# S5's matrices B turned by eight transposes of 128 rows, turned feed-forward rows copied out of PSUM first, and the last product in banks of its own

## The chip, the core and the metric

The kernel runs on one core of a Trainium2 chip. The core has five engines that run side by side and wait for each other through semaphores: TensorE (PE in the profile; its weight loads are listed apart as PEld) multiplies and transposes and writes to PSUM, ScalarE (ACT) and VectorE (DVE) work elementwise on PSUM and on the on-chip memory SBUF, GpSimd (POOL) works elementwise on SBUF and issues transfers, and SyncE (SP) issues transfers. PSUM has eight banks; a bank holds 512 float32 values in each of 128 partitions. The metric is the time of one execution on the device, in microseconds (us); lower is better.

## What is computed

One encoder layer in float32: 512 tokens of 1024 channels, 256 memory tokens, a feed-forward width of 2816. Cut to what matters here:

```python
def s5_scan(u, lam_re, lam_im, log_step, b_re, b_im, c_re, c_im, reverse):
    ...
    b = lax.complex(b_re.astype(f32), b_im.astype(f32))
    b_bar = ((lam_bar - 1.0) / lam)[..., None] * b
    bu = jnp.einsum('gpc,lbgc->lbgp', b_bar, u.astype(jnp.complex64))
    ...

def reference(...):
    ...
        n = rms_norm(h, mix_norm_g[i])
        proj = n @ w_in[i]
        ya = s5_branch(...)          # S5, two directions, 32 groups, 64 states, 16 channels
        yb = sgu_branch(...)
        merged = gate_a * (ya @ w_proj_a[i]) + gate_b * (yb @ w_proj_b[i])
        h = h + merged @ w_out[i]
        h = h + memory_cross_attention(rms_norm(h, xattn_norm_g[i]), memn, ...)
        h = h + swiglu(rms_norm(h, ffn_norm_g[i]), w_gate[i], w_up[i], w_down[i])
    return rms_norm(h, final_norm_g)
```

S5's matrices B come as `b_re` and `b_im` of shape (2 directions, 32 groups, 64 states, 16 channels); `swiglu` is `(silu(hn @ w_gate) * (hn @ w_up)) @ w_down`.

## The kernel before

Everything is float32 but runs through TensorE in a faster format in two parts: `split` (line 83) makes of a matrix a high part `hi` (a cast by ScalarE, line 85) and a low part `lo` (source minus `hi`, VectorE, line 86), and each product is three matmuls: hi*hi, hi*lo, lo*hi (`mm3`, line 371). Weights come in blocks of 512 KB from a list, `plan`: loaded by SyncE three and more blocks ahead into three buffers `raw` (line 145 and others), split two blocks ahead into three buffers each of `whi` and `wlo`. A large part of the big products is done by a scheme with seven half-size products (numbered `q` = 1 to 7, weights and activations added up beforehand).

Order. The program is written as one stream. When it is built, a planner that simulates a timeline of the engines (`schedule_with_timeline_sim=True`) puts the instructions of each engine into an order; each engine and each transfer queue then works in that fixed order. Where the code says `in_order` (or sets `pinned`), the order written stands. Small jobs are put between the products by `later` and by a generator `s5_program`, which `tick` moves on.

PSUM is two pools: five banks `mm` for products (`bank`), three banks `aux` for small results and transposes (`aux`), each handed out in turn.

Three places matter here.

**S5's setup** (`s5_setup`, from line 688), early in the kernel while the first product (`pt`, token rows times `w_in`) runs. `brow` holds B with 64 rows (real and imaginary part, 32 groups) of direction, state and channel; for each of the 16 channels one transpose (line 726) turns 64 rows by 128 columns (a step of 16 elements between the columns) into 128 by 64, eight to a bank `pbc`, and ScalarE copies each bank to `raw_b` (line 727). The loads of `brow` (line 716) stand in SyncE's queue ahead of those of `crow` (C's matrices, line 720) and of the next blocks of `w_in` (line 145).

**The turning of rows for the feed-forward part.** After the attention's output product (`pt`, lines 1664 to 1688), each of the four row blocks of 128 tokens is normalised (`scale_row`, giving `xs`; the factor `r` is a power taken on GpSimd, line 511) and turned by `turn_row`, which calls `to_feat` (line 528): per half (`q` = 0, 1) four transposes into one `aux` bank `ptr` (line 534), then `split` from that bank into `fn_hi` and `fn_lo`, then ScalarE copies the bank to `full` (line 540). `full` is later used to add up activations for the products 5, 6 and 3. For rows 0 and 1 the transposes are `turned`: they stand in the written order between the products of rows 2 and 3, in the loop of lines 1684 to 1686. There are four half rows for three banks, so the second half of row 1 uses the bank of the first half of row 0.

**The last product and the output.** The down product (`w_down`) runs in the order q = 1, 5, 2, 6, 3, 7, 4 (`DOWN`, line 260), each in six chunks of weights, in two banks `dx`, `dq` or `dv` for the two row blocks of a half of the tokens. `onto_h` (line 1931) adds a finished pair of banks onto the residual `h`. Products 1, 6, 7 and 4 pile up in `dx`: after product 7, `onto_h(dx, 2, 0, SUBTRACT)` (line 1953) takes `dx` off the first column half of rows 2 and 3, and product 4 goes on adding into the same banks, which later go onto their second half (line 1971 for row 2; `seed_last`, line 1900, for row 3). The first three chunks of product 4 do both rows; the last three (`held`) do row 2, then row 3 in two parts of 256 columns. Finished halves are multiplied by the gain ahead of time into `hg` (four rows of 512, in `rest`; `first_half`, line 1874), so that at the end only one factor per token is left: for the last row `write` (line 1915) scales 512 columns on ScalarE and stores them from SyncE's queue (line 1924), and scales the other 512, which lie in `h`, on VectorE and stores them from ScalarE's queue (lines 1926 and 1929).

Of the kernel before, what the change touches and what calls it, by code (L numbers as in the profile page):

```python
# [9 lines left out]
F32 = mybir.dt.float32  # L10
F32R = mybir.dt.float32r
AF = mybir.ActivationFunctionType
ALU = mybir.AluOpType
# [4 lines left out]
P = 128  # L18
D = 1024
T = 512  # L20
NT = T // P
# [5 lines left out]
G = 32  # L27
C = 16
# [24 lines left out]
def hybrid_layer_kernel(  # L53
# [8 lines left out]
    nc = tc.nc  # L62
# [17 lines left out]
    def aux(name, shape=(P, 512)):  # L80
        return pa.tile(list(shape), F32, tag="aux", name=name)

    def split(dst_hi, dst_lo, src):

        hi = nc.scalar.copy(dst_hi, src)  # L85
        lo = nc.vector.tensor_tensor(dst_lo, src, dst_hi.bitcast(F32), ALU.subtract)  # L86
        if pinned[0]:
            in_order(hi)
            in_order(lo)
        return hi  # L90
# [434 lines left out]
        for i in range(2):  # L525
            nc.vector.scalar_tensor_tensor(dst[:, HALF[i]], src[:, HALF[i]], r, g[:, HALF[i]], ALU.mult, ALU.mult)

    def to_feat(src, hi, lo, tsl, full=None, skip=None, part=(0, 1), turned=False):

        for q in part:  # L530
            ps = aux("ptr", (P, 4, P))
            for j in range(4):
                k = 4 * q + j
                m = nc.tensor.transpose(ps[:, j, :], src[:, k * P:(k + 1) * P], ident)
                if turned:
                    in_order(m)
            if q != skip:
                split(hi[:, 4 * q:4 * q + 4, tsl], lo[:, 4 * q:4 * q + 4, tsl], ps)
            if full is not None:
                nc.scalar.copy(full[:, 4 * q:4 * q + 4, tsl], ps)  # L540

    xsp = [None]
# [145 lines left out]
    def s5_setup():  # L688
# [22 lines left out]
        yield 0.3  # L711


        brow = s5p.tile([2 * G, 2, 64, C], F32, tag="u", name="brow")
        for i, src in enumerate((s5_b_re, s5_b_im)):
            nc.sync.dma_start(brow[G * i:G * i + G], src[0].rearrange("d g p c -> g d p c"))
        crow = s5p.tile([P, 2, C // 4, 2, 64], F32, tag="tt", name="crow")
        for i, src in enumerate((s5_c_re, s5_c_im)):
            for d in range(2):
                nc.sync.dma_start(crow[:, i, :, d, :], src[0, d].rearrange("g (a b) p -> (g a) b p", a=4))  # L720
        bb = s5p.tile([P, 2, G, C], F32, tag="raw_b", name="raw_b")
        rows = brow.rearrange("g d p c -> g (d p) c")
        for n in range(2):
            ps = aux("pbc", (P, C // 2, 2 * G))
            for k in range(C // 2):
                nc.tensor.transpose(ps[:, k, :], rows[:, :, 8 * n + k], ident[:2 * G, :2 * G])
            A_.copy(bb.rearrange("p i g c -> p c (i g)")[:, 8 * n:8 * n + 8, :], ps)
            yield None
        cc = s5p.tile([P, 2, G, C], F32, tag="raw_c", name="raw_c")
        for i in range(2):  # L730
# [921 lines left out]
    scaled = {}  # L1652
# [3 lines left out]
        rms_scale(h[:, t, :], g_f, xs, ss)  # L1656

    def turn_row(t, turned=False):
        to_feat(scaled.pop(t), fn_hi, fn_lo, slice(t * P, (t + 1) * P), full, turned=turned)

    fin = add_evac(1, 1, scale_row)
    held, ps = [], {}
# [197 lines left out]

    g_o = gain(final_norm_g, "g_o")
    hg = rest[0][:, 4:8, :]
    msq = fp.tile([P, NT + 2], F32, name="msq", bufs=1)

    def mean_sq(dst, ss, base):
# [4 lines left out]
    def first_half(t, half):  # L1870

        early[t] = half
        sum_sq(hss[:, 2, t, half:half + 1], h[:, t, HALF[half]])
        nc.vector.tensor_tensor(hg[:, t, :], h[:, t, HALF[half]], g_o[:, HALF[half]], ALU.mult)
        nc.vector.tensor_scalar(msq[:, t:t + 1], hss[:, 2, t, half:half + 1], 1.0 / D, EPS, ALU.mult, ALU.add)

    def inv_root(t, ss):
        r = np_.tile([P, 1], F32, tag="r", name="r", bufs=2)
        ms = np_.tile([P, 1], F32, tag="ms", name="ms", bufs=2)
        root = nc.scalar.activation(ms, ss, AF.Sqrt, bias=msq[:, t:t + 1], scale=1.0 / D)  # L1880
        inv = nc.vector.reciprocal(r, ms)
        if pinned[0]:
            in_order(root)
            in_order(inv)
        return r
# [14 lines left out]
    def seed_last(ps):  # L1900
        for i in range(2):
            in_order(nc.vector.tensor_tensor(last[i], h[:, NT - 1, last_cols[i]], ps[:, 256 * i:256 * i + 256], ALU.add))

    def finish_last(i):
        ss = np_.tile([P, 2], F32, tag="ss", name="ss", bufs=2)
        sum_sq(ss[:, 0:1], last[i])
        in_order(nc.vector.tensor_tensor(h[:, NT - 1, last_cols[i]], last[i], g_o[:, last_cols[i]], ALU.mult))
        if i == 0:
            mean_sq(msq[:, NT:NT + 1], ss[:, 0:1], msq[:, NT - 1:NT])
        else:  # L1910
            write(NT - 1, inv_root(NT, ss[:, 0:1]))

    stores = []

    def write(t, r):
        rows = out[t * P:(t + 1) * P]
        cs, hs = HALF[early[t]], HALF[1 - early[t]]
        scaled = nc.scalar.activation(hg[:, t, :], hg[:, t, :], AF.Copy, scale=r)
        if t < 2:
            nc.vector.scalar_tensor_tensor(h[:, t, hs], h[:, t, hs], r, g_o[:, hs], ALU.mult, ALU.mult)  # L1920
            stores.extend([(rows[:, cs], hg[:, t, :]), (rows[:, hs], h[:, t, hs])])
            return
        in_order(scaled)
        nc.sync.dma_start(rows[:, cs], hg[:, t, :])
        if t == NT - 1:
            in_order(nc.vector.tensor_scalar(h[:, t, hs], h[:, t, hs], r, None, ALU.mult))
        else:
            in_order(nc.vector.scalar_tensor_tensor(h[:, t, hs], h[:, t, hs], r, g_o[:, hs], ALU.mult, ALU.mult))
        (nc.scalar if t == NT - 1 else nc.sync).dma_start(rows[:, hs], h[:, t, hs])

    def onto_h(ps, t0, half, op):
        for t in range(2):
            hs = h[:, t0 + t, HALF[half]]
            nc.vector.tensor_tensor(hs, hs, ps[t], op)  # L1934
# [16 lines left out]
        finish(t)  # L1951
    down_product(dx, 7, False)
    onto_h(dx, 2, 0, ALU.subtract)
    for t in range(2, 4):
        first_half(t, 0)

    held = []
    for c in range(CHUNKS):
        ops_ = next_w(w_down, 4, c)
        if c == CHUNKS - 1 - LOADS:  # L1960
            for dst, src in stores:
                in_order(nc.sync.dma_start(dst, src))
# [48 lines left out]
```

## Time and profile before

| | us |
|---|---|
| median of 3 runs | 864.61 (863.97 to 865.8) |
| the profiled execution, whole | 865.88 |
| its span, first to last instruction | 864.1 |
| around the span | 1.8 |

| transfers in the profiled execution | |
|---|---|
| moved | 170.09 MB, mean 197 GB/s |
| SyncE's queue | 140.07 MB, 49.3% of 16 engines' span |
| GpSimd's queue | 28.55 MB, 20.4% |

How to read it: PE, DVE, ACT, POOL are the engines, PEld TensorE's weight loads, SPq, ACTq, POOLq the queues of transfers. A row of the timeline is start and duration in us, engine, line, operation, output and inputs, shapes, count; several like instructions are merged to one row with their count, and a bracket says how long the engine had been idle and what ended that. Matmuls overlap: one that is listed with 0.39 us is followed by the next after 0.23 us, so a row's start against the next row's start is the cost. The granted clock of TensorE is 0.999 of full over the whole span.

### The profile page before, as it was taken

How to read it: one execution, taken by the hardware profiler on the slowest of the kernel's cores; microseconds unless marked ns; L12 is line 12 of the kernel's file. 1: busy time of each engine (PE TensorE's matmuls, PEld its weight loads, DVE VectorE, ACT ScalarE, POOL GpSimd, SP SyncE). 2: the span in 40 equal slices, each digit the busy share in tenths (PEclk: the TensorE clock that was granted, in tenths of full speed). 3: DMA queues.
4: the chain of work that ended last, by engine and by line, in shares of the span. 5: the costliest groups of instructions: out<-in, count | busy, mean ns of one | idle time of the engine just before them, and what ended most of it. 6: DMA issues, size and time to landing. Idle time of an engine off the chain costs nothing.

```text
span 864.1 us, 14763 instructions
## 1 busy us (share of the span) xinstructions
PE 855.3 (99%) x5776; PEld 766.1 (89%) x5776; DVE 662.2 (77%) x1077; ACT 465.9 (54%) x698; POOL 88.4 (10%) x119
## 2 busy tenths in 40 slices
PE   9999999999999999999999999999999999999997
PEld 7888888888889988899899887999999999988886
DVE  7698999899646867678758655867877768899875
ACT  6734863244445544457557544645545454655674
POOL 0002211211021110010010001001211111000000
PEclk9999999999999999999999999999999999999999
DMA  8759576988574798635696455557899898366664
GB/s 271 191 166 315 100 216 157 234 201 208 139 220 157 248 308 267 218 112 197 214 273 169 130 160 134 146 167 182 207 241 231 213 229 219 96 192 205 199 187 155
DMA packets 116041, 170.09 MB, mean 197 GB/s; under 512 B 9458, under 2 KB 80642, under 8 KB 115843
## 3 DMA queue, kind: packets, MB, share of 16 engines
q1 hardware_dynamic: 95618, 140.07, 49.3%
q0 software_dynamic: 20064, 28.55, 20.4%
q8 instruction: 45, 0.74, 0.3%
q10 hardware_dynamic: 288, 0.52, 0.2%
q14 instruction: 26, 0.21, 0.1%
HBM read 160.23 MB, written 48.73 MB: 242 GB/s over the span
## 4 chain that ended last, share of the span: by engine, by line
PE 96%; DVE 1%; DMA 1%; issue 0%; ACT 0%; POOL 0%; SPq 0%; POOLq 0%; ACTq 0%
PE pf L374 27%; PE pt L374 15%; PE px L1250 13%; PE dx L374 7%; PE pq L1250 6%; PE dq L374 3%; PE pv L1250 3%; PE bx L1250 3%; PE qx L1250 3%; PE dv L374 2%; PE pz L958 2%; PE qv L1250 1%; PE po L374 1%; PE psc L374 1%; PE py L1014 1%; PE qq L1250 1%
## 5 line engine op out<-in xcount | busy, mean ns | idle before, releaser
L85 ACT CAST whi<-wraw 128x1024 fp32r<-128x1024 f32 x141 | 145.3, 1030 | 163.9 <-PE pf L374 56.3
L86 DVE TENSOR_TENSOR wlo<-wraw,whi 128x1024 fp32r<-128x1024 f32 x141 | 168.4, 1196 | 59.7 <-ACT whi L85 58.9
L374 PE MATMUL pf<-xn,whi 128*128 128x512 f32 x448 | 139.6, 392 | 0.0
L374 PEld LDWEIGHTS pf<-xn,whi 128*128 128x128 f32 x448 | 83.5, 188 | 16.7
L374 PE MATMUL pf<-xn,wlo 128*128 128x512 f32 x224 | 87.8, 392 | 0.0
L1250 PE MATMUL px<-fn,whi 128*128 128x256 f32 x480 | 83.4, 277 | 0.0
L1250 PEld LDWEIGHTS px<-fn,whi 128*128 128x128 f32 x480 | 72.5, 188 | 0.2
L86 DVE TENSOR_TENSOR wlo<-b,whi 128x1024 fp32r<-128x1024 f32 x40 | 49.0, 1224 | 26.0 <-ACT whi L85 26.0
L85 ACT CAST whi<-b 128x1024 fp32r<-128x1024 f32 x40 | 42.2, 1054 | 48.7 <-PE px L1250 27.8
L1250 PE MATMUL px<-fn,wlo 128*128 128x256 f32 x240 | 66.4, 277 | 0.0
L1250 PE MATMUL pq<-s,whi 128*128 128x256 f32 x320 | 55.0, 276 | 0.0
L374 PE MATMUL dx<-whi,s 128*128 128x512 f32 x166 | 52.2, 391 | 0.4 <-DVE h L1934 0.4
L86 DVE TENSOR_TENSOR wlo<-t,whi 128x1024 fp32r<-128x1024 f32 x30 | 36.7, 1225 | 18.4 <-ACT whi L85 18.4
L85 ACT CAST whi<-t 128x1024 fp32r<-128x1024 f32 x30 | 31.6, 1054 | 34.2 <-PE pv L1250 11.4
L374 PEld LDWEIGHTS pf<-xn,wlo 128*128 128x128 f32 x224 | 42.0, 188 | 8.9 <-issue 0.2
L1250 PEld LDWEIGHTS pq<-s,whi 128*128 128x128 f32 x320 | 48.2, 188 | 0.0
L1250 PEld LDWEIGHTS px<-fn,wlo 128*128 128x128 f32 x240 | 45.1, 188 | 0.0
L1250 PE MATMUL pq<-s,wlo 128*128 128x256 f32 x160 | 44.2, 276 | 0.0
L374 PE MATMUL pt<-whi,xn 128*128 128x512 f32 x128 | 43.1, 403 | 0.0
L374 PEld LDWEIGHTS dx<-whi,s 128*128 128x128 f32 x166 | 31.1, 188 | 7.4 <-ACT whi L85 0.8
L374 PE MATMUL dx<-wlo,s 128*128 128x512 f32 x83 | 32.1, 389 | 0.0
L289 POOL DMA_DIRECT2D dsum<-in_w_down_dram x12 | 13.2, 1104 | 173.0 <-DMA dsum<-in_w_down_dram 169.3
(457 smaller groups left out, 2223.8 us busy)
## 6 DMA issues: line engine op xcount, KB each, us to landing
wraw<-in_w_in_dram SPq DMA_DIRECT2D x34, 512.0 KB, 4.7
dsum<-in_w_down_dram SPq DMA_DIRECT2D x20, 512.0 KB, 5.5
wraw<-dsum SPq DMA_DIRECT2D x20, 512.0 KB, 3.9
b<-in_w_gate_dram SPq DMA_DIRECT2D x15, 512.0 KB, 6.7
b<-in_w_up_dram SPq DMA_DIRECT2D x15, 512.0 KB, 5.7
wraw<-in_w_down_dram SPq DMA_DIRECT2D x15, 512.0 KB, 4.9
dsum<-in_w_down_dram POOLq DMA_DIRECT2D x10, 512.0 KB, 7.9
dsum<-dsum POOLq DMA_DIRECT2D x10, 512.0 KB, 8.0
```

The costliest lines, as they stand in the source:

```text
L85: hi = nc.scalar.copy(dst_hi, src)
L86: lo = nc.vector.tensor_tensor(dst_lo, src, dst_hi.bitcast(F32), ALU.subtract)
L289: plan[j + step][1].append((0, lambda d=dst, x=more: nc.gpsimd.dma_start(d, x, accum_op=ALU.add)))
L374: m = nc.tensor.matmul(ps, a[x], b[y], start=start and i == 0, stop=stop and i == 2, skip_group_check=free)
L958: nc.tensor.matmul(ps[:, g, :], wt[:, g, :], u[:, o * GO + g, :], start=True, stop=True)
L1014: in_order(nc.tensor.matmul(ps[64 * j:64 * j + 64, :, :, h, :].rearrange("p q d c -> p d q c"), a, b, start=k == ks[0], stop=k == ks[2], t ...
L1250: nc.tensor.matmul(ps[:, j, :], a[x], b[y], start=start and j == k == i == 0, stop=k == 3 and i == 2, skip_group_check=True)
```

## The change

1. `brow` gets 128 rows: 64 as before, and 64 with the same data shifted by 8 channels (two more loads, each of 32 rows with two directions of 4,064 bytes instead of 4,096). One transpose then turns channel c (from the first 64 rows) and channel c + 8 (from the others): eight transposes of 128 by 128, four to a bank. ScalarE's two copies keep their size and write the same elements.
2. `to_feat` gets a switch `copied`, set for the feed-forward rows: ScalarE copies the bank to `full` first, and `split` reads `full`, in SBUF, not the bank.
3. Product 4 starts afresh in `dq`, whose last reader was `onto_h(dq, 0, 0, ADD)`; what product 7 left in `dx` is added to the second half of rows 2 and 3 by two more additions, `onto_h(dx, 2, 1, ADD)`.
4. The rows of `hg` are permuted, so that both halves of the last row lie side by side in it (`last_row`, the places 1 and 2; place 2 held half of row 0 until its store). The last scaling is cut at column 352: ScalarE does 352 columns, VectorE 672.

```diff
-    def to_feat(src, hi, lo, tsl, full=None, skip=None, part=(0, 1), turned=False):
+    def to_feat(src, hi, lo, tsl, full=None, skip=None, part=(0, 1), turned=False, copied=False):
...
+            src_ = ps
+            if full is not None and copied:
+                src_ = full[:, 4 * q:4 * q + 4, tsl]
+                nc.scalar.copy(src_, ps)
             if q != skip:
-                split(hi[:, 4 * q:4 * q + 4, tsl], lo[:, 4 * q:4 * q + 4, tsl], ps)
-            if full is not None:
+                split(hi[:, 4 * q:4 * q + 4, tsl], lo[:, 4 * q:4 * q + 4, tsl], src_)
+            if full is not None and not copied:
                 nc.scalar.copy(full[:, 4 * q:4 * q + 4, tsl], ps)
...
-        brow = s5p.tile([2 * G, 2, 64, C], F32, tag="u", name="brow")
-        for i, src in enumerate((s5_b_re, s5_b_im)):
-            nc.sync.dma_start(brow[G * i:G * i + G], src[0].rearrange("d g p c -> g d p c"))
+        brow = s5p.tile([P, 2, 64 * C], F32, tag="u", name="brow")
+        for c0 in range(0, C, C // 2):
+            for i, src in enumerate((s5_b_re, s5_b_im)):
+                first = (2 * c0 // C * 2 + i) * G
+                nc.sync.dma_start(brow[first:first + G, :, 0:64 * C - c0],
+                                  src[0].rearrange("d g p c -> g d (p c)")[:, :, c0:64 * C])
...
-        rows = brow.rearrange("g d p c -> g (d p) c")
+        rows = brow.rearrange("r d (p c) -> r (d p) c", c=C)
         for n in range(2):
-            ps = aux("pbc", (P, C // 2, 2 * G))
-            for k in range(C // 2):
-                nc.tensor.transpose(ps[:, k, :], rows[:, :, 8 * n + k], ident[:2 * G, :2 * G])
-            A_.copy(bb.rearrange("p i g c -> p c (i g)")[:, 8 * n:8 * n + 8, :], ps)
+            ps = aux("pbc", (P, C // 4, P))
+            for k in range(C // 4):
+                nc.tensor.transpose(ps[:, k, :], rows[:, :, 4 * n + k], ident)
+            A_.copy(bb.rearrange("p i g (h k) -> p k h (i g)", h=2)[:, 4 * n:4 * n + 4],
+                    ps.rearrange("p k (h x) -> p k h x", h=2))
             yield None
...
-        to_feat(scaled.pop(t), fn_hi, fn_lo, slice(t * P, (t + 1) * P), full, turned=turned)
+        to_feat(scaled.pop(t), fn_hi, fn_lo, slice(t * P, (t + 1) * P), full, turned=turned, copied=True)
...
     hg = rest[0][:, 4:8, :]
+    HG = (2, 3, 0, 1)
+    last_row = hg[:, 1:3, :].rearrange("p a c -> p (a c)")
+    CUT = 352
...
-        nc.vector.tensor_tensor(hg[:, t, :], h[:, t, HALF[half]], g_o[:, HALF[half]], ALU.mult)
+        nc.vector.tensor_tensor(hg[:, HG[t], :], h[:, t, HALF[half]], g_o[:, HALF[half]], ALU.mult)
...
-        in_order(nc.vector.tensor_tensor(h[:, NT - 1, last_cols[i]], last[i], g_o[:, last_cols[i]], ALU.mult))
+        in_order(nc.vector.tensor_tensor(last_row[:, last_cols[i]], last[i], g_o[:, last_cols[i]], ALU.mult))
...
-            write(NT - 1, inv_root(NT, ss[:, 0:1]))
+            write_last(inv_root(NT, ss[:, 0:1]))
...
+    def write_last(r):
+        rows = out[(NT - 1) * P:NT * P]
+        x, y = last_row[:, 0:CUT], last_row[:, CUT:D]
+        in_order(nc.scalar.activation(x, x, AF.Copy, scale=r))
+        in_order(nc.vector.tensor_scalar(y, y, r, None, ALU.mult))
+        nc.sync.dma_start(rows[:, 0:CUT], x)
+        nc.scalar.dma_start(rows[:, CUT:D], y)
...
     onto_h(dx, 2, 0, ALU.subtract)
+    onto_h(dx, 2, 1, ALU.add)
     for t in range(2, 4):
         first_half(t, 0)
...
-            rows_product(dx, 4, c, ops_, (0, 1), slice(0, 512), False, c == CHUNKS - HELD - 1)
+            rows_product(dq, 4, c, ops_, (0, 1), slice(0, 512), c == 0, c == CHUNKS - HELD - 1)
...
-    seed_last(dx[1])
+    seed_last(dq[1])
...
-        rows_product(dx, 4, c, ops_, (0,), slice(0, 512), False, c == CHUNKS - 1, True)
+        rows_product(dq, 4, c, ops_, (0,), slice(0, 512), False, c == CHUNKS - 1, True)
...
-    in_order(nc.vector.tensor_tensor(h[:, 2, HALF[1]], h[:, 2, HALF[1]], dx[0], ALU.add))
+    in_order(nc.vector.tensor_tensor(h[:, 2, HALF[1]], h[:, 2, HALF[1]], dq[0], ALU.add))
```

More of the change, by code (lines that the diff above doesn't have):

```diff
@@ L1917, in write @@
         cs, hs = HALF[early[t]], HALF[1 - early[t]]
-        scaled = nc.scalar.activation(hg[:, t, :], hg[:, t, :], AF.Copy, scale=r)
+        hgt = hg[:, HG[t], :]
+        scaled = nc.scalar.activation(hgt, hgt, AF.Copy, scale=r)
         if t < 2:
             nc.vector.scalar_tensor_tensor(h[:, t, hs], h[:, t, hs], r, g_o[:, hs], ALU.mult, ALU.mult)
-            stores.extend([(rows[:, cs], hg[:, t, :]), (rows[:, hs], h[:, t, hs])])
+            stores.extend([(rows[:, cs], hgt), (rows[:, hs], h[:, t, hs])])
             return
         in_order(scaled)
[L1924 to L1929, printed above, removed]
+        nc.sync.dma_start(rows[:, cs], hgt)
+        in_order(nc.vector.scalar_tensor_tensor(h[:, t, hs], h[:, t, hs], r, g_o[:, hs], ALU.mult, ALU.mult))
+        nc.sync.dma_start(rows[:, hs], h[:, t, hs])
+    def write_last(r):
[5 more added lines that the diff above has]
+        nc.scalar.dma_start(rows[:, CUT:D], y)
     def onto_h(ps, t0, half, op):
```

## The prediction

> **What bounds the kernel now.** I read the head of the page first, then what TensorE waited for, then the timeline at each of the places that the change touches.
>
> ```profile
> span 864.1 us, 14763 instructions
> PE 855.3 (99%) x5776; PEld 766.1 (89%) x5776; DVE 662.2 (77%) x1077; ACT 465.9 (54%) x698; POOL 88.4 (10%) x119
> PE ptr L534 <- ACT full L540: 1.2, 1, 1.2
> PE dx L374 <- DVE h L1934: 0.4, 1, 0.4
> ```
>
> TensorE is busy for 99% of the span and none of the others comes near. So what takes an instruction off TensorE, or a wait, counts in full, and a saving on ScalarE or VectorE counts for nothing unless TensorE waits for it. The last two rows are the only waits of TensorE behind the first 20 us that this view lists: one where rows are turned for the feed-forward part (line 534, for ScalarE's copy to `full`), one where product 4 wants the banks that VectorE is still reading (line 1934). The change touches both, the short transposes of the setup, and the output's tail.
>
> **Part 1, the transposes of B.**
>
> ```profile
> 9.58 0.31 SPq L716 DMA_DIRECT2D brow<-in_s_b_re_dram  x1
> 11.07 0.31 SPq L716 DMA_DIRECT2D brow<-in_s_b_im_dram  x1
> 12.46 0.60 SPq L720 DMA_DIRECT2D crow<-in_s_c_re_dram  x1
> 14.85 0.39 SPq L145 DMA_DIRECT2D wraw<-in_w_in_dram  x1
> 23.04 0.38 SPq L145 DMA_DIRECT2D wraw<-in_w_in_dram  x1
> 27.58 1.05 ACT L85 CAST whi<-wraw 128x1024 fp32r<-128x1024 f32 x1 [1.89 <-PE pt L374]
> 29.24 1.97 PE L726 MATMUL pbc<-ident,brow 64*128 64x64 f32 x16
> 31.14 0.66 PE L733 MATMUL pbc<-ident,crow 128*128 128x128 f32 x4
> 31.55 0.48 PE L374 MATMUL pt<-whi,xn 128*128 128x512 f32 x1
> 33.27 1.05 ACT L85 CAST whi<-wraw 128x1024 fp32r<-128x1024 f32 x1
> brow<-in_s_b_im_dram SPq DMA_DIRECT2D x1, 256.0 KB, 5.7
> ```
>
> From start to next start, the sixteen transposes of 64 rows take 31.14 - 29.24 = 1.90, 0.12 each; four of 128 rows right behind them take 31.55 - 31.14 = 0.41, 0.10 each. A transpose of twice the rows thus costs no more, and eight take 0.82 at that rate, 0.95 if the step of 16 elements between columns keeps them at 0.12. The gain is 0.95 to 1.08; I take **1.0**. As a lower bound I allow 0.16 for each, the four of the row at 31.14 spread over its whole 0.66: then 0.6 are left. ScalarE's copies of the two banks keep their size.
>
> The two added loads go into SyncE's queue, which takes 1.4 to 1.5 from one `brow` load to the next (9.58, 11.07, 12.46). They would stand at about 12.5 and 13.9, and what comes behind, the loads of `crow` and the `w_in` block at 14.85, would go out 2.8 later. Landing takes 5.7, so the shifted rows are there at about 20, nine before the transposes at 29.24. The block of 14.85 is cast only at 27.58, when TensorE has freed a buffer, and the one of 23.04 only at 33.27. That is room enough for 2.8 of queue; I put the loads at nothing, and at what they cost without this cover in the first rival.
>
> **Part 2, `full` copied first.**
>
> ```profile
> 526.42 1.04 PE L534 MATMUL ptr<-ident,xs 128*128 128x128 f32 x8
> 527.22 0.47 PE L374 MATMUL pt<-whi,ot_hi 128*128 128x512 f32 x1
> 528.06 1.06 ACT L85 CAST fn<-ptr 128x512 fp32r<-128x512 f32 x2
> 528.68 0.54 POOL L511 TENSOR_TENSOR r<-ms,mhalf 128x1 f32<-128x1 f32 x1 [3.40 <-DVE ms L510]
> 529.00 1.06 ACT L85 CAST whi<-b 128x1024 fp32r<-128x1024 f32 x1
> 529.26 1.42 DVE L526 SCALAR_TENSOR_TENSOR xs<-h,r,g_f 128x512 f32<-128x512 f32 x2 [0.73 <-POOL r L511]
> 530.07 0.66 PE L534 MATMUL ptr<-ident,xs 128*128 128x128 f32 x4
> 530.60 1.28 DVE L86 TENSOR_TENSOR fn<-ptr,fn 128x512 fp32r<-128x512 f32 x2
> 531.31 0.59 ACT L540 COPY full<-ptr 128x512 f32<-128x512 f32 x1 [1.25 <-DVE fn L86]
> 531.95 0.66 PE L534 MATMUL ptr<-ident,xs 128*128 128x128 f32 x4 [1.23 <-ACT full L540]
> 532.36 0.71 PE L374 MATMUL pt<-s,ot_hi 128*128 128x512 f32 x2
> 537.92 0.40 PE L374 MATMUL pf<-fn,s 128*128 128x256 f32 x2
> ```
>
> Row 0's first bank is cast by ScalarE at 528.06, but VectorE takes its `lo` from it only at 530.60, because it makes row 1's `xs` first, and the copy to `full` starts when that `lo` ends (1.25 idle, ended by VectorE's `fn`). The bank is free at 531.90, and only then the second half of row 1 can be turned. With the copy first, the bank is free after one copy of 0.59: at 528.7 if ScalarE takes it where it now takes the cast (528.06), at 529.7 if the cast of 1.06 comes before it. Both are ahead of 530.5.
>
> What is late next is `xs`: VectorE ends its second half at 529.26 + 1.42 = 530.68, and the four transposes read it. So they start at about 530.72 and not at 531.95; from there four take 532.36 - 531.95 = 0.41 as now. The gain is **1.23**. If there were no wait left at all, the eight would take 527.22 - 526.42 = 0.80 in place of 532.36 - 530.07 = 2.29, a gain of 1.49; that is the upper bound.
>
> What it costs: `lo` now waits for two operations of ScalarE, not one, so it comes 0.59 later for each half row. The first product that needs it is `pf` at 537.92, at 536.7 with the wait gone, and it reads first halves of rows 0 and 1 only. Row 1's first half is turned by 530.5; one operation left over from row 0, a cast of 1.06, then `full` and `hi` (3 x 0.59 + 1.06 = 2.8) put its `hi` at 533.3, its `lo` 0.64 (half of 1.28) later at 534.0, and there are 2.7 left. Number and size of ScalarE's and VectorE's instructions stay the same.
>
> A rule speaks against this part. The Trainium skill (SBUF — State Buffer, Who interferes with whom) says that a VectorE instruction with two inputs in SBUF contends with a GpSimd instruction that reads SBUF; the `lo` becomes one. By that rule GpSimd's power `r` could be held for the length of a `lo`. The row at 529.26 shows VectorE idle for 0.73 for that very `r`, so the two do not meet today, and no row here shows what would come of it. What a held `r` would cost is worked out among the rivals.
>
> **Part 3, product 4 in `dq`.**
>
> ```profile
> 842.08 0.39 PE L374 MATMUL dx<-wlo,s 128*128 128x512 f32 x1
> 842.27 0.69 DVE L1934 TENSOR_TENSOR h<-h,dx 128x512 f32<-128x512 f32 x1
> 842.30 0.39 PE L374 MATMUL dx<-whi,s 128*128 128x512 f32 x1
> 843.11 0.47 PE L374 MATMUL dx<-whi,s 128*128 128x512 f32 x1 [0.42 <-DVE h L1934]
> 845.21 1.22 DVE L86 TENSOR_TENSOR wlo<-wraw,whi 128x1024 fp32r<-128x1024 f32 x1
> ```
>
> and from the chain of waits, in order of time:
>
> ```profile
> 797.81 14.96 PE dx L374 x66
> ```
>
> Matmuls follow each other by 842.30 - 842.08 = 0.22; the first of product 4 comes 0.81 after the last of product 7, when VectorE has read the bank (842.96). In `dq` nothing is being read, and the gain is 0.81 - 0.22 = 0.59; I take **0.6**. The two added additions are 2 x 0.69 = 1.38 on VectorE just then. Behind them in its queue stands `wlo` of the third chunk (845.21 to 846.43), wanted when two chunks of twelve matmuls are through: 842.53 + 24 x 0.227 (14.96 / 66 in the chain's row) = 848.0. With 1.38 in front it ends at 847.8, just in time, and with a gain product (0.69) planned ahead as well at 848.5, a wait of 0.5. So the bounds are 0.1 and 0.6; I take 0.6, since the additions are wanted only by `seed_last`, much later, and the list as planned now already puts `wlo` ahead of unhurried work.
>
> **Part 4, the tail.**
>
> ```profile
> 859.61 0.72 ACT L1918 ACTIVATE rest<-rest,r 128x512 f32<-128x512 f32 x1 [0.23 <-DVE r L1881]
> 859.61 0.49 DVE L1926 TENSOR_SCALAR h<-h,r 128x512 f32<-128x512 f32 x1
> 860.13 0.35 ACTq L1929 DMA_DIRECT2D out_dram<-h  x1
> 860.36 0.33 SPq L1924 DMA_DIRECT2D out_dram<-rest  x1
> DMA to landing us min/median/max: 2.1/2.5/3.7
> ```
>
> If all of a scaling's time goes by columns, ScalarE's takes 0.72 x 352/512 = 0.50 and VectorE's 0.49 x 672/512 = 0.64; if none does, 0.72 and 0.49. SyncE's store goes out up to 0.22 earlier, ScalarE's up to 0.15 later, and that one then carries 336 KB, not 256. The later landing sets the end. I take **0**, between a gain of 0.2 and a loss of 0.2. The wait on row 0's store, for the place in `hg`, is long over.
>
> **Sum.** 1.0 + 1.23 + 0.6 + 0 = 2.83. From the profiled execution, 865.88 (span 864.1 and 1.8 around it), that gives 863.05. This execution was 1.27 above the median of the runs, 864.61, so for the median I say **861.8**.
>
> **The rivals.** For the first, a row of SyncE's queue and one of the busy times by stretches (10 to 20 us; the last columns are granted clock, share of the transfer engines and GB/s):
>
> ```profile
> 30.09 1.96 SPq L145 DMA_DIRECT2D wraw<-in_w_in_dram  x2
> 10.00:20.00 10.00, 9.71 (x51) 7.37 (x51) 9.72 (x20) 8.10 (x22) 0.00 (x0) 1.00 0.95 261
> ```
>
> *Slower: TensorE waits for the shifted B.* The place is SyncE's queue between 11 and 32. If the planner sets the two new loads behind the `w_in` blocks that wait for a buffer, behind 30.09 + 1.96 in the row here, they land at 32.05 + 5.7 = 37.8, and TensorE, which works in order, stands from 29.24 on: 8.5 lost, 864.61 + 8.5 - 2.8 = 870.3. It decides once a load goes out after 29.24 - 5.7 = 23.5. For it: the queue is planned by a simulated time and the transfers are busy here (0.95 from 10 to 20). Against it: the first two went out twelve ahead of that.
>
> *The wait moves to `xs`.* If VectorE is planned to take row 0's `lo` before row 1's `xs`, it stands until `hi` (now second on ScalarE, ending at 528.06 + 2 x 0.59 = 529.24), and `xs` comes a `lo` of 0.64 later: 0.6 of part 2 are left, 1.0 + 0.6 + 0.6 = 2.2, 862.4.
>
> *Part 3 is given back by the late `wlo`.* Then 1.0 + 1.23 + 0.1 = 2.3, 862.3; together with the rival before, 1.0 + 0.6 + 0.1 = 1.7, 862.9.
>
> *The change doesn't free the bank.* If the copy is planned behind the casts, or both `lo` of row 0 (1.28) come ahead of `xs`, part 2 brings nothing: 1.6, 863.0.
>
> *GpSimd's `r` is held by a `lo`.* One `lo` of 0.64 late on `xs` while TensorE comes to turn that row: 2.83 - 0.64 = 2.2, 862.4. The page on SBUF named above is the reason to list it.
>
> **How the numbers follow.** Forecast 0.60; the wait at `xs` 0.12; late `wlo` alone 0.08; both, or the bank not freed, 0.08; `r` held 0.04; slower 0.08. A measurement here tells 0.2%, 1.7 us, from no change; faster therefore means below 862.9, slower above 866.3. Of the forecast some 0.57 falls below that, of the three cases at 862.3 and 862.4 (0.24) some 0.17, as the runs spread by 0.6 and more about their median: faster 0.74. Slower is 0.08, the rest, 0.18, no difference. The range: the upper bounds give 1.08 + 1.49 + 0.6 + 0.2 = 3.4, 861.2, less the 0.6 by which the lowest run lay under the median, 860.6; upwards it reaches over the case at 863.0, with 0.6 for part 1 in place of 1.0 and the 0.7 of a run's spread on top, 864.1. Outside are the slower case and some few in a hundred.
>
> **What would show it.** Part 1 is right if eight transposes stand in place of sixteen and take 0.8 to 1.0 to the next start, with no wait of TensorE for a transfer before 60. Part 2 is right if the row `PE ptr <- ACT full` is gone and the second half of row 1 starts with the end of `xs`; wrong if TensorE waits there for another `fn`, or at `pf` for a `lo`. Part 3 is right if the first matmul into `dq` follows by 0.22, and wrong if a wait for `wlo` shows in the chunks behind. The whole is wrong if TensorE shows waits at places that the diff does not touch, since then the planner has laid the order differently.

## The result, and the profile after

| | us | runs |
|---|---|---|
| before | 865.61 (863.97 to 868.01) | 22 |
| after | 863.55 (862.43 to 866.08) | 22 |
| ratio | 0.9979, interval 0.9971 to 0.9986 | |
| after, second set (e16) | 865.35 (862.84 to 868.11) | 12 |
| before beside it | 865.21 (864.2 to 870.71) | 34 |
| ratio there | 0.9995, interval 0.998 to 1.0009 | |

In the first set the change makes the kernel 1.8 faster (1.2 to 2.5, the ratio times 865.6). In the second, with the same program, no gain can be told (the interval reaches from 1.7 faster to 0.8 slower): nine of its twelve executions took 864.96 or more, where four of the first set's 22 did. So two things have to be explained: what the profile of the first set shows, and what made the long executions of the second.

The profiled execution of the first set took 863.27. Its head, and what TensorE waited for (us in total, times, longest):

```profile
span 861.5 us, 14748 instructions
PE 854.4 (99%) x5768; PEld 765.6 (89%) x5768; DVE 662.8 (77%) x1079; ACT 465.2 (54%) x698; POOL 89.2 (10%) x119
PE pt L577 <- DVE ones L493: 1.1, 1, 1.1
PE ptr L639 <- issue: 0.2, 1, 0.2
PE ptr L639 <- DVE ms L622: 0.2, 1, 0.2
```

The two rows of before at lines 534 and 374 are gone; those left lie in the first 20 us. The timeline at the places of the change:

```profile
7.53 0.60 PE L639 MATMUL ptr<-ident,xt 128*128 128x128 f32 x4
...
15.85 0.47 SPq L722 DMA_DIRECT2D brow<-in_s_b_im_dram  x1
...
26.31 6.07 SPq L145 DMA_DIRECT2D wraw<-in_w_in_dram  x3
...
29.48 1.05 PE L733 MATMUL pbc<-ident,brow 128*128 128x128 f32 x8
30.28 0.47 PE L374 MATMUL pt<-whi,xn 128*128 128x512 f32 x1
...
32.59 1.05 ACT L85 CAST whi<-wraw 128x1024 fp32r<-128x1024 f32 x1
...
74.94 1.09 PE L959 MATMUL pw<-ident,wsx 128*128 128x128 f32 x8
...
527.20 1.05 ACT L540 COPY full<-ptr 128x512 f32<-128x512 f32 x2
528.14 1.15 ACT L85 CAST fn<-full 128x512 fp32r<-128x512 f32 x2
528.40 1.41 DVE L526 SCALAR_TENSOR_TENSOR xs<-h,r,g_f 128x512 f32<-128x512 f32 x2 [0.73 <-POOL r L511]
529.21 1.38 PE L534 MATMUL ptr<-ident,xs 128*128 128x128 f32 x8
529.73 1.28 DVE L86 TENSOR_TENSOR fn<-full,fn 128x512 fp32r<-128x512 f32 x2
530.34 0.70 PE L374 MATMUL pt<-s,ot_hi 128*128 128x512 f32 x2
...
840.42 0.39 PE L374 MATMUL dx<-whi,s 128*128 128x512 f32 x1
840.47 1.28 DVE L1951 TENSOR_TENSOR h<-h,dx 128x512 f32<-128x512 f32 x2
840.65 0.62 PE L374 MATMUL dq<-whi,s 128*128 128x512 f32 x2
...
857.04 0.59 ACT L1943 ACTIVATE rest<-rest,r 128x352 f32<-128x352 f32 x1 [0.24 <-DVE r L1892]
857.04 0.57 DVE L1944 TENSOR_SCALAR rest<-rest,r 128x672 f32<-128x672 f32 x1
```

Start against next start, as in the prediction: eight transposes of B take 30.28 - 29.48 = 0.80 where sixteen took 1.90, 1.10 less. The eight of row 1 take 530.34 - 529.21 = 1.13 where they took 2.29, 1.16 less; the two copies to `full` run first, one right after the other, and what is left is the wait for `xs`, which ends at 528.40 + 1.41 = 529.81. Product 4 follows by 840.65 - 840.42 = 0.23, where the gap was 0.81: 0.58 less. From the last scalings to the end of the span 861.5 - 857.04 = 4.46 are left, where it was 864.1 - 859.61 = 4.49. Together 2.87. The spans differ by 2.6; the 0.3 between them were lost before the change begins, as the first transposes start at 7.53 here and at 7.20 before (its row stands in the next section).

### The profile page after: what moved, and what is told of

The parts are those of the page before. It is cut to its first block, busy times and chain, and to the rows that moved or that the text cites. A ratio compares the mean times of both kernels' runs of the same rounds, so it can differ in the third digit from the quotient of the medians.

```text
span 861.5 us, 14748 instructions
## 1 busy us (share of the span) xinstructions
PE 854.4 (99%) x5768; PEld 765.6 (89%) x5768; DVE 662.8 (77%) x1079; ACT 465.2 (54%) x698; POOL 89.2 (10%) x119
## 4 chain that ended last, share of the span: by engine, by line
PE 99%; DVE 0%; ACT 0%; issue 0%
PE pf L374 27%; PE pt L374 18%; PE px L1258 13%; PE pq L1258 6%; PE dx L374 5%; PE dq L374 5%; PE pv L1258 3%; PE bx L1258 3%; PE qx L1258 3%; PE dv L374 2%; PE pz L966 2%; PE qv L1258 1%; PE po L374 1%; PE psc L374 1%; PE py L1022 1%; PE qq L1258 1%
## 5 line engine op out<-in xcount | busy, mean ns | idle before, releaser
L374 PE MATMUL dx<-whi,s 128*128 128x512 f32 x132 | 41.4, 390 | 0.0
L374 PE MATMUL dq<-whi,s 128*128 128x512 f32 x122 | 38.1, 389 | 0.0
L500 ACT ACTIVATE sq<-h 128x512 f32<-128x512 f32 x23 | 14.5, 630 | 29.3 <-DVE h L1448 24.1
```

The lines of the kernel that those rows point to most:

```text
L374: m = nc.tensor.matmul(ps, a[x], b[y], start=start and i == 0, stop=stop and i == 2, skip_group_check=free)
L500: act = nc.scalar.activation(sq[:, :src.shape[-1]], src, AF.Square, bias=bias, accum_out=dst)
```

## The experiments

**The same program, and each part alone.** e1 is the kernel before, unchanged. The others take one part's lines of the diff. e3 takes the four loads of part 1 and still turns 64 rows at a time; e6 is part 2 with the split left on the bank:

```diff
 # e6, in to_feat
             if full is not None and copied:
-                src_ = full[:, 4 * q:4 * q + 4, tsl]
-                nc.scalar.copy(src_, ps)
+                nc.scalar.copy(full[:, 4 * q:4 * q + 4, tsl], ps)
 # e3, in s5_setup: brow and its four loads as after, the sixteen transposes of before
-        rows = brow.rearrange("g d p c -> g (d p) c")
+        rows = brow.rearrange("r d (p c) -> r (d p) c", c=C)[0:2 * G]
 # e7, the loop and the three places behind it
-            rows_product(dx, 4, c, ops_, (0, 1), slice(0, 512), False, c == CHUNKS - HELD - 1)
+            rows_product(dq, 4, c, ops_, (0, 1), slice(0, 512), c == 0, c == CHUNKS - HELD - 1)
```

> The kernel before, unchanged, against itself. Both theories: ratio 1.000 with an interval of some 0.07% each way, and a span of 863 to 866 us. What it shows is how far the same program's span and its first 10 us differ from run to run: the two profiles so far differ by 0.34 us at the first transposes (7.20 and 7.53), before anything that was changed has run. If that is the start of TensorE's clock and not the change, this profile's first transposes lie anywhere from 7.2 to 7.6.

> Only part 1 (shifted rows of B, eight transposes). Theory A (the steps add up; the runs' smaller gain is scatter): TensorE reaches the S5 kernels and everything behind 1.0 to 1.3 us earlier, no wait for a transfer, ratio 0.9986 (1.2 us), and the waits of 1.2 at line 534 and 0.4 at product 4 stay. Theory B (the added loads cost the start something in the common run that the one profile did not show): the ratio is 0.9995 to 1.001 while the row of eight transposes still takes 0.8 to 0.9.

> The four loads of brow with 128 rows, but turned as before by sixteen transposes of the first 64 rows; the shifted rows are loaded and not used. Theory A: ratio 1.000, loads of w_in that follow go out up to 2.8 us later and no engine waits for them. Theory B: 0.5 to 1.5 us slower, 1.0006 to 1.0017, with a wait for a transfer or later rows of x in the first 30 us.

> The changed kernel with part 1 undone. Theory A: 1.2 + 0.6 = 1.8 to 1.9 us faster than before, ratio 0.9979, both waits of TensorE gone. Theory B: the same for this kernel, so that it alone is as fast as the whole change (0.9979) and part 1 adds nothing.

> Only part 2 (full copied first, split from full). By the forecast 1.2 us faster, ratio 0.9986: the second half of row 1 starts 0.04 us behind the second half of xs, with a stop of TensorE of 0.2 to 0.3 us left. Rival (the lo that now waits for two operations of ScalarE comes late at the first feed-forward product): the stop at line 534 goes and one of 0.5 us or more shows at pf or px, ratio 0.9993 or more.

> As part 2, but split goes on reading the PSUM bank; only the order of the three readers changes (copy to full, hi, lo). Theory: the wait is VectorE's lo standing behind xs while it still has to read the bank. Then the bank is free when row 0's first lo ends (about 0.6 us earlier than before, since the copy no longer follows it), and half of the 1.2 us is left as a wait, ended by VectorE's fn: 0.6 us faster, ratio 0.9993. Rival (it was the copy's place behind lo): the whole 1.2 us goes, ratio 0.9986.

> Only part 3 (product 4 in dq, two more additions). By the forecast 0.6 us faster, ratio 0.9993: the first matmul into dq follows by 0.22 and wlo of the later chunks is in time. Rival (the two additions of 0.69 push wlo back): a stop of TensorE of 0.3 to 0.9 us between the chunks, ratio 1.000.

> Only part 4 (last row in hg, cut at 352). By the forecast no difference, 1.000, with the two last stores issued within 0.05 us of each other and their landing 0.2 us earlier or later at most. Rival: the larger store from ScalarE's queue lands last and costs 0.2 us or more.

| | median (lowest to highest) | ratio to before, interval |
|---|---|---|
| e1, before again | 865.56 (864.36 to 866.58) | 1.0 (0.9991 to 1.0008) |
| e2, part 1 | 867.97 (863.86 to 870.41) | 1.0024 (1.0011 to 1.0038) |
| e3, the loads of part 1 | 865.51 (864.67 to 868.78) | 1.0005 (0.9994 to 1.0015) |
| e4, parts 2, 3 and 4 | 864.12 (863.69 to 865.7) | 0.9987 (0.9978 to 0.9996) |
| e5, part 2 | 864.55 (864.11 to 868.29) | 0.9997 (0.9987 to 1.0008) |
| e6, part 2, split from the bank | 865.12 (864.45 to 868.17) | 1.0003 (0.9993 to 1.0012) |
| e7, part 3 | 864.55 (863.8 to 865.46) | 0.9992 (0.9983 to 1.0001) |
| e8, part 4 | 865.24 (863.84 to 867.13) | 1.0002 (0.9993 to 1.0011) |

Part 3 has the forecast's size (0.7, with 0.6 forecast), though its interval reaches to no change; of part 4 nothing can be told. Parts 2 to 4 together bring 1.1 (0.3 to 1.9) where 1.83 were forecast. The surprise is part 1: alone it makes the kernel 2.1 slower (1.0 to 3.3). Seven of its twelve executions took 867.9 to 870.4, the others 863.9 to 866.2. The added loads alone (e3) cost nothing that can be told. The parts do not add up to the whole: 2.1 lost and 1.1 won would leave 1.0 lost, where the whole change won 1.8 in its first set and nothing that can be told in its second. How often an execution is a long one differs between sets.

**Where part 1 loses.** e9 and e10 are e2's kernel, looked at again.

> Part 1 alone, the same kernel as before, for a second profiled execution; it may be one of those that take 868 to 870 (7 of 12 did). Theory: such an execution loses 3 to 5 in one long stop of TensorE, and it lies where GpSimd's queue holds r behind the accumulating load of t (TensorE's wait for xs or full at 525 to 531). First rival: the stop is the wait of pw for VectorE's nm at 83, which was 1.5 in one profile. Second rival: it is in the first 40 us, at the rows of x or at B, because four loads take the transfer engines' time. If the execution is one of the short ones (863.9 to 866.2), none of the three shows and nothing is told.

> Part 1 alone a third time, for the same question and with the same three expectations; two executions that both take 868 or more and stop at one place would settle where, and two that stop at different places would say that part 1 alone has no single place.

They took 867.72 and 866.32. What TensorE of e9 waited for, and then e9's timeline:

```profile
PE ptr L534 <- ACT full L540: 1.2, 1, 1.2
PE pt L573 <- DVE ones L493: 1.1, 1, 1.1
PE pw L955 <- DVE wsx L980: 1.0, 1, 1.0
PE pz L962 <- DVE zh L968: 0.9, 1, 0.9
```

```profile
27.55 4.84 SPq L145 DMA_DIRECT2D wraw<-in_w_in_dram  x3
33.74 1.05 ACT L85 CAST whi<-wraw 128x1024 fp32r<-128x1024 f32 x1 [1.12 <-DMA wraw<-in_w_in_dram]
37.11 0.23 ACT L753 ACTIVATE slab<-slab 128x32 f32<-128x32 f32 x1
37.37 0.23 DVE L765 TENSOR_TENSOR pows<-slab 128x32 f32<-128x32 f32 x1 [1.31 <-ACT slab L753]
74.78 1.22 DVE L980 TENSOR_TENSOR wsx<-wsx,etmp 128x1024 f32<-128x1024 f32 x1
76.06 1.09 PE L955 MATMUL pw<-ident,wsx 128*128 128x128 f32 x8 [1.04 <-DVE wsx L980]
83.12 1.23 DVE L866 TENSOR_TENSOR e<-raw_c,pe 128x1024 f32<-128x1024 f32 x1 [3.47 <-DMA ed<-e]
91.38 1.89 PE L962 MATMUL pz<-u,wt 128*128 128x64 f32 x15 [0.93 <-DVE zh L968]
```

Read it upwards from 76.06. There TensorE comes to transposes of S5's inputs (`pw`, in `s5_inputs`) and has waited 1.04 for VectorE's `wsx`. VectorE is late because its S5 work began late, at 37.37, with powers that ScalarE prepares at 37.11; and ScalarE was late because its cast at 33.74, which stands ahead in its queue, had waited 1.12 for the landing of a `w_in` block. That block had gone out at 27.55, behind the two added loads. e10 has the same chain, with 0.98 at the cast and 0.56 at `pw`. The theory put down with these runs, one long stop at GpSimd's queue at 525, thus falls, and so does the wait for `nm`; its second rival was nearest, but the loss shows 40 us later than it said.

This chain is not the whole loss of e9. Its span is 2.8 longer than that of e2's profile (866.0 and 863.2): 0.3 of that is there at the first transposes, 1.1 comes at this `pw`, 1.1 at the `pz` of 91.38 (88.90 in e2), and 0.3 at transposes of `pw` at 123. The last two stops are ended by VectorE's `zh`; before the first of them VectorE had stood 3.47 for a store of `e` to memory, where it stood 1.54 in e2. e10 and e12 below have a stop of 0.84 for `zh` at 123 too. How much of these later stops comes from the late block, and how much from the store, no run takes apart.

The places of the chain in the profile before, and in that of e2 (865.02):

```profile
7.20 0.60 PE L635 MATMUL ptr<-ident,xt 128*128 128x128 f32 x4
32.10 1.14 ACT L734 COPY raw_c<-pbc 128x512 f32<-128x512 f32 x1
73.63 1.23 DVE L976 TENSOR_TENSOR wsx<-wsx,etmp 128x1024 f32<-128x1024 f32 x1
76.18 1.09 PE L951 MATMUL pw<-ident,wsx 128*128 128x128 f32 x8
```

```profile
26.55 5.54 SPq L145 DMA_DIRECT2D wraw<-in_w_in_dram  x3
32.14 1.06 ACT L85 CAST whi<-wraw 128x1024 fp32r<-128x1024 f32 x1
33.09 1.08 ACT L738 COPY raw_c<-pbc 128x512 f32<-128x512 f32 x1
74.66 1.09 PE L955 MATMUL pw<-ident,wsx 128*128 128x128 f32 x8
```

Before, `wsx` ended at 74.86 and TensorE came at 76.18: 1.3 of room. With part 1 TensorE comes 1.1 earlier, and 0.58 of room is left in e2 (`wsx` ends at 74.08), 0.44 in the profile after. If the block lands in time, as in these two, nothing is lost here; each late microsecond beyond that room is a stop at `pw`.

The rows show one thing more. Before, ScalarE copies `raw_c` at 32.10 and casts the block behind it, at 33.27. In every kernel with part 1 the planner has put the cast ahead of that copy, so that it comes earlier by the 1.1 of the copy and a late block holds up the copy as well. With the order of before, e3 casts at 33.24 without a wait, though its block went out at 27.19. In e9 that order would have put the cast at about 33.7 (the copies of `raw_b` end at 32.62, and the copy of `raw_c` takes 1.10), which is when the block was there; this is an estimate. No run keeps the cast behind the copy, so how the loss divides between the queue and the new order stays open.

**r off GpSimd.** The first theory's own test: `r` by a square root on ScalarE and a reciprocal on VectorE, in the kernel before (e11) and in the changed one (e12).

```diff
-        nc.gpsimd.tensor_tensor(r, ms, mhalf, ALU.pow)
+        nc.scalar.activation(ms, ms, AF.Sqrt)
+        nc.vector.reciprocal(r, ms)
```

> The kernel before, with the factor r of the feed-forward rows made by a square root on ScalarE and a reciprocal on VectorE, not by GpSimd's power, so that it no longer stands behind GpSimd's accumulating load of t. Theory (the wait at line 534 is there or not as that load comes late or early): the wait is gone in the profile, xs starts within 1.0 of VectorE's ms in place of 2.4, and the median is lower than before's by part of 1.2: 864.6 to 865.2. Rival (the wait comes from the order on VectorE and ScalarE, not from r): TensorE still waits 1.0 or more for full, and the time is within 0.3 of before's. A square root not yet loaded on ScalarE could cost some 1 to 1.5 there; it shows as idle of ScalarE ahead of it.

> The changed kernel with the same edit. Theory: in it the wait at line 534 is gone already, so r off GpSimd brings at most the 0.26 that TensorE still stops for xs: 863.3 to 863.6, and the spread of its runs (862.4 to 866.1) is narrower by the late loads of t. Rival: the runs at 865 and above come from elsewhere (start or layer norm), and the spread stays.

865.44 (0.9998, 0.999 to 1.0007) and 863.65 (0.9978, 0.9969 to 0.9987; highest 865.96): no gain over before in e11, none over the changed kernel's first set (863.55) in e12, and the spread of e12 stays. In e11 TensorE's wait at the copy to `full` is halved (0.64); a load of the root's table, shown here, takes the place of what `r` waited for:

```profile
523.30 1.28 ACT L512 ACT_TABLE_LOAD   x1 [0.46 <-DVE ms L510]
531.47 0.66 PE L538 MATMUL ptr<-ident,xs 128*128 128x128 f32 x4 [0.64 <-ACT full L544]
```

e12's profile shows the chain found in e9 in the changed kernel too: the cast at 34.46 had waited 1.80 for the block, `pw` 1.42 for `wsx`.

**The pushed-back block, taken away in two ways.** e13 is part 1 without its added loads; it leaves out the upper eight channels of B, whose rows are zero. e14 keeps them, but puts four loads of the gating unit, which stand in SyncE's queue ahead of that `w_in` block, behind it (`behind(a, b)` fixes the order, a after b); e15 does the same in the changed kernel, and e16 is the changed kernel beside it.

```diff
 # e13
-        for c0 in range(0, C, C // 2):
+        nc.gpsimd.memset(brow[2 * G:P, :, :], 0.0)
+        for c0 in (0,):
 # e14, e15 (block 7 of w_in; likewise for both loads of gbr and for mix)
-    nc.sync.dma_start(wsr, sgu_w[0].rearrange("h t s -> t h s"))
+    behind(nc.sync.dma_start(wsr, sgu_w[0].rearrange("h t s -> t h s")), w_in_loads[7])
```

> Part 1 alone without its two added loads: the upper 64 rows of brow are set to zero by GpSimd, so the upper eight channels of B are left out; transposes and copies stay. Theory (the added loads push the next w_in block back in SyncE's queue, ScalarE's cast of it waits for the landing, and VectorE's chain of S5 comes late to pw): the long runs of part 1 alone are gone, no wait of pw for wsx in the profile, ScalarE's cast behind raw_b has no idle ended by a transfer, median 864.3 to 864.9 (part 1's 1.1 in place). Rival (TensorE merely comes earlier to a chain on VectorE that is late anyhow): the waits at pw stay and the median is 866 or more, as in part 1 alone.

> Part 1 alone with all four loads of B, but with the four loads of the gating unit (wsx, gbr twice, mix: 1 MB, wanted only after 85) behind the w_in block in SyncE's queue, not ahead of it. Theory: that block goes out some 2.8 earlier, the cast does not wait for it, and the median is 864.3 to 864.9 where part 1 alone had 868. Rival (the transfer engines are the limit, not the place in the queue, or the chain on VectorE is late anyhow): 866 or more.

> The changed kernel with the same four loads behind the w_in block. Theory: its runs of 865 and 866 are gone, the spread goes from 3.6 to about 2, and the median is 862.6 to 863.2, 0.3 to 0.9 under the changed kernel beside it. Rival: the same as the changed kernel within 0.2.

> The changed kernel again, beside the one with the loads moved. Theory: 863.3 to 863.8, a few of eleven runs at 865 or more, and whichever run is profiled has a stop at pw if its block of w_in landed after ScalarE was through with raw_b, and none if before.

| | median (lowest to highest) | ratio to before, interval |
|---|---|---|
| e13, part 1 without the loads | 865.86 (863.69 to 866.79) | 0.9997 (0.9987 to 1.0006) |
| e14, part 1, loads behind | 865.2 (864.51 to 866.32) | 0.9997 (0.9988 to 1.0005) |
| e15, changed, loads behind | 863.42 (862.91 to 864.21) | 0.9978 (0.9969 to 0.9987) |
| e16, changed | 865.35 (862.84 to 868.11) | 0.9995 (0.998 to 1.0009) |

The profile of e16 (868.11), then that of e15 (863.94):

```profile
PE pw L959 <- DVE wsx L984: 2.5, 1, 2.5
...
27.20 5.23 SPq L145 DMA_DIRECT2D wraw<-in_w_in_dram  x3
35.02 1.05 ACT L85 CAST whi<-wraw 128x1024 fp32r<-128x1024 f32 x1 [2.36 <-PE pt L374]
76.85 1.23 DVE L984 TENSOR_TENSOR wsx<-wsx,etmp 128x1024 f32<-128x1024 f32 x1
78.13 1.43 PE L959 MATMUL pw<-ident,wsx 128*128 128x128 f32 x8 [2.48 <-DVE wsx L984]
81.07 0.63 PE L374 MATMUL pt<-wlo,xn 128*128 128x512 f32 x1
82.27 0.39 PE L374 MATMUL pt<-wlo,xn 128*128 128x512 f32 x1
```

```profile
23.81 0.38 SPq L147 DMA_DIRECT2D wraw<-in_w_in_dram  x1
32.66 1.07 ACT L85 CAST whi<-wraw 128x1024 fp32r<-128x1024 f32 x1
73.39 1.23 DVE L988 TENSOR_TENSOR wsx<-wsx,etmp 128x1024 f32<-128x1024 f32 x1
75.20 1.09 PE L963 MATMUL pw<-ident,wsx 128*128 128x128 f32 x8
```

In e16 the cast waits 2.36, and `pw` 2.48. The bracket names TensorE; but TensorE ran to the same plan in the first profile of this kernel, where the cast started at 32.59 without any wait, so what is late must be the other thing that the cast needs, the block; its landing is not recorded. The span is 4.8 longer than in that first profile, and three things make it up. TensorE stops 0.49 at 74.59 and 2.48 at `pw`; the cast's 2.36, with 1.04 that VectorE stood at 72.09 for a store of `e`, less the 0.44 of room, makes 2.96, and the two stops together are 2.97. The rest is the clock: right behind the long stop, from 78.75 on, the clock granted to TensorE is 0.50 of full for 3.41, which costs 1.7. The rows show it: eight transposes of `pw` take 1.43 where they took 1.09, and a matmul 0.63 at 81.07 and 0.39 again at 82.27. In the other profiles with a late block the stops are 1.42 and shorter and the granted clock stays at full. In e15 the block goes out at 23.81, the cast does not wait, and no execution was above 864.21, where nine of the twelve of e16 took 864.96 or more. That is 1.9 between the medians, by the order of five transfers. The levels were not those expected: e15 is 0.2 above its range, and e16 1.6 above. So the place of these loads ahead of the block is what made the long executions here; that they also need the cast ahead of the copy of `raw_c` is neither shown nor excluded.

e13 and e14 lose the long executions of part 1 alone (none above 866.8, where seven of twelve were), but their medians, 865.86 and 865.2, lie between what the theory and its rival had said. The rival holds in part, and so part 1's 1.1 was not won even without the late block. e14's profile (866.32) shows a second way in which VectorE comes late:

```profile
81.57 1.23 DVE L870 TENSOR_TENSOR e<-raw_c,pe 128x1024 f32<-128x1024 f32 x1 [3.20 <-DMA ed<-e]
89.86 2.00 PE L966 MATMUL pz<-u,wt 128*128 128x64 f32 x16 [0.42 <-DVE zh L972]
```

VectorE stands 3.20 for a store of `e` out to memory, and TensorE waits at 89.86. All twenty profiles have that wait of VectorE, 0.9 to 4.0 long, 2.53 in the profile before, where TensorE does not stop for it. In e8, which has only the tail changed, it is 3.97 long (the bracket names TensorE, where seventeen of the profiles name the store) and TensorE stands 1.50 right behind it:

```profile
81.47 1.23 DVE L862 TENSOR_TENSOR e<-raw_c,pe 128x1024 f32<-128x1024 f32 x1 [3.97 <-PE pt L374]
85.11 1.06 PE L951 MATMUL pw<-ident,wsx 128*128 128x128 f32 x8 [1.50 <-DVE nm L1135]
```

**Do the moved loads help by themselves?** e17 moves them in the kernel before, e18 is e15 again.

> The kernel before with the gating unit's four loads behind the w_in block. There ScalarE casts that block only 4 us after it has landed, so theory: the place of the loads is worth nothing by itself, within 0.3 of before, and what the changed kernel won by it was part 1's gain kept. Rival (the earlier block helps any kernel): 0.5 to 1.9 under before, and no stop of pw at 72 to 123 us where before has one in some executions.

> The changed kernel with the loads behind, once more and beside e17. Theory: 862.6 to 863.6 and no run above 865, as in e15; 1.6 to 2.2 under before. Rival (e15 had a lucky set of executions): half of the runs at 865 and above, as the changed kernel had in e16.

865.13 (0.9999, 0.999 to 1.0007) and 863.72 (0.9981, 0.9972 to 0.999; highest 864.96). Moving the loads is worth nothing in the kernel before; in the changed one it holds the gain, on two chips: beside the changed kernel it was 1.9 faster (e15 and e16), and against that kernel's first set, 863.55, it is level and narrower (864.96 at most, where that had 866.08).

## Why the prediction was right, and where it was wrong

*Parts 2, 3 and 4 went as worked out.* In the profile part 2 gave 1.16 for 1.23, and the stop that is left is the one named, `xs`; part 3 gave 0.58 for 0.59, and no `wlo` was late; part 4 gave 0.03. e7, part 3 alone, shows the same 0.23 (841.46 to 841.69). Of the rivals, the wait at `xs` from a `lo` planned first, the late `wlo`, the bank not freed and the held `r` did not come: the `lo` of row 0 starts at 529.73, with `xs` all but done. As `r` had ended before `xs` began at 528.40, no `lo` ran beside it, and the rule of the Trainium skill (SBUF — State Buffer, Who interferes with whom) was not put to the test.

*Part 2's size in the medians stays open.* Of eleven profiles with the order of before at line 534 and `r` on GpSimd, nine show the wait of 1.1 to 1.2, one of 0.6 and one, e1's, none, so on average 1.0 was there to take. e5 measured 0.3 (-0.7 to 1.1); its median is 0.65 under that of before beside it, 865.2. e6, the split from the bank, can't be told from e5, and in its profile the wait is gone as well; as the transposes come only at 531.27 there, it does not tell which reader had held the bank.

*Part 1 was right on TensorE* (1.10 for 1.0) *and wrong in its cover*, and this is the step that failed: "That is room enough for 2.8 of queue; I put the loads at nothing". With them part 1 alone is 2.1 slower (e2), where 1.0 faster was forecast. The room was read from a cast at 33.27: 23.04 + 2.8, and the 6.2 that this block took to land there, make 32.0, with 1.2 to spare. Three things were missed. The block went out later than that: at 26.31, 26.55, 26.77, 27.20, 27.47 and 27.55 in the profiles of after, e2, e10, e16, e12 and e9, where the kernels with the loads of before have 23.04 to 25.87 (e5), so that the 23.04 of the prediction was the earliest of them. The cast came forward, to 32.59 after and 32.14 in e2, because the planner now puts it ahead of the copy of `raw_c`. And what stands behind the cast was not followed: ScalarE's and VectorE's S5 work down to `pw`, which had 1.3 of room before and has 0.4 to 0.6 with part 1. Six profiles have part 1's transposes with its loads in their planned place: in two the block was in time, in four the cast waited 0.98, 1.12, 1.80 and 2.36, and TensorE then 0.56, 1.04, 1.42 and 2.48 at `pw`.

*The first rival had the right place and the wrong victim.* It looked in SyncE's queue between 11 and 32, but for the shifted B, which came in time (no wait at line 733), and from a threshold of 23.5 for its loads, which went out by 15.9. What arrived late was what they pushed back. The last sentence of the prediction said that waits at places the diff does not touch would show it wrong, since the planner would then have laid the order differently. They came, at `pw`, and ScalarE's order had been laid differently; the landing had to be late as well.

*Sizes.* The sum was 2.83; profile against profile (865.88 and 863.27) it is 2.6, the medians of the first set are 2.06 apart, those of the second not at all. The forecast also stood on the three runs shown, whose median, 864.61, is 1.0 below that of the 22 runs: of the 1.75 between 861.8 and 863.55, that is the larger part.

*Open.* Why the block is there within 5.6 of its issue in e2 and, by its cast, only after 7.8 in e16, and whether the second set differs from the first by its chip (that of the first is not on record) or by chance; e12, the changed kernel but for `r`, has the gain on another chip than e16. What keeps e13 at 865.86: its one profile shows no wait at `pw`.

## What to carry to other kernels

When an edit lets the busiest engine come earlier, look for what it meets next: every chain on another engine that ended "just in time" may now be the bound, and the slack that is left after the edit (here 0.4 to 0.6 of 1.3) is what a late transfer may take. Look also at the order in which each engine now does its work: an edit on one engine can move a reader on another. For a load added to a queue, check the transfers behind it, when their readers will read them after the edit, and what is queued behind those readers; then move behind them what is wanted latest. And profile the same program more than once: the first profile of the changed kernel showed every forecast gain in place, and the waits that take them back came in other executions.

## What the runs showed of the hardware

The same start differs between executions before anything of the change has run: the first transposes start between 6.61 (e15) and 7.59 (e14) in the twenty profiles. The Trainium skill (TensorE: Matmul & The Clock Gate, Part 1) says that the warm-up of TensorE's clock (its rise to full speed) follows a free-running window and differs from run to run; the traces agree: in their record of the granted clock, full speed begins between 4.89 (e15) and 7.09 (e14), 6.29 in the profile before and 6.97 in that after, and the later it begins, the later those transposes start, to within 0.02. So a difference of 0.3 between two profiles is not yet one of the kernels.

A stop of TensorE can cost more than its length: behind the 2.48 of e16 the granted clock was 0.50 for 3.41, and 1.7 more went. No stop of 1.50 (e8) or less had that in these profiles, and none between was seen.

A transpose of 128 rows costs no more than one of 64: 0.80 / 8 = 0.10 against 1.90 / 16 = 0.12, with the same step of 16 elements between the columns.
